# Widening the vector block behind x from 66 to 80 columns, so that what follows it in SBUF starts at a multiple of 64 bytes

## The chip, the cores and the metric

The kernel runs on one core of one Trainium2 chip. Its time is the device time of one execution in microseconds; the time before is the median of three executions. A profiled execution on the same core gives the trace that all readings come from. The core's engines are TensorE (PE, with its weight loads listed apart as PEld), VectorE (DVE), ScalarE (ACT), GpSimd (POOL) and SyncE (SP, which issues nearly all DMAs).

## The reference, cut to what matters

One decoder layer on x of 512 tokens by 1024 channels, all in float32: a half-step SwiGLU feed-forward block, a mixer that runs a gated linear recurrence and a stick-breaking attention side by side, and a second feed-forward block.

```
x = x + 0.5 * swiglu(rms_norm(x, ffn1_norm), w_gate, w_up, w_down)      # 1024 -> 2816 -> 1024
h = rms_norm(x, mix_norm);  proj = h @ w_in                              # 1024 -> 2560
y_rnn = rg_lru(...);        y_att = stick_breaking(q, k, v)              # 8 heads of 64
x = x + concat(norm(y_rnn), norm(y_att)) @ w_out                         # 1024 -> 1024
x = x + 0.5 * swiglu(rms_norm(x, ffn2_norm), w_gate, w_up, w_down)
```

## The kernel before

x is kept transposed: eight tiles `x0` to `x7` of 128 channels by 512 tokens. All small vectors (norm gains, convolution weights, biases) stand as columns in one block `vec`, which shares the first tile with x's first block: `x0` is 512 + `NVEC` float32 columns wide (lines 121 to 123) and comes with one DMA (line 547).

Products of float32 accuracy are made from parts. A matrix W is split on the chip into a high part, rounded to the float32r type by ACT, and a low part, the rest, by DVE (`weights` and `parts`, lines 126 to 136). An activation is split in the same way (`Normed.add` for x's parts `xh` and `xl`, `split` for the hidden layer's `hh` and `hl`). One product is then three matmuls into the same accumulator (`mm3`, lines 142 to 145):

```
nc.tensor.matmul(out_, wh, ah, start=start, stop=False)
nc.tensor.matmul(out_, wh, al, start=False, stop=False)
return nc.tensor.matmul(out_, wl, ah, start=False, stop=stop)
```

Each matmul loads a stationary operand of 128 columns (PEld) and streams a moving operand of 512, 384, 256 or 128 columns past it (PE).

The stages in order of time:

- `first_products` (lines 532 to 587): gate and up products of the first three column blocks of the first feed-forward block. Its weights have buffers of their own (`first_r`, `first_h`, `first_l`), all from a pool that opens behind x's parts. For each k, six matmuls follow each other with the same moving part of x and six weights into six accumulators: 3 x 8 x 6 = 144 matmuls at line 580.
- `ffn` (lines 221 to 522), called for "a" and "b". Column blocks 0 to 5 are plain (`products`, through `mm3`; "a" makes only three there). The other 16 blocks are made in pairs by `fast`: a Strassen-like scheme of seven half products (`matrix`, `product`, line 397), whose moving operand is 256 columns wide, or 512 for some of the matmuls where the pair is "wide" (`WIDE`, line 38). A narrow matrix has 7 x 12 matmuls of 256 columns, a wide one 7 x 4 of 512 and 7 x 4 of 256. Each of the two blocks has ten wide and six narrow matrices. `down` multiplies by the third weight matrix in chunks of 6, 6, 6 and 4 blocks; eight down blocks of 18 matmuls stand between the half products of the next pairs (`BETWEEN`, line 34) for the second and third chunk, the others stand by themselves. The last down block of "b" is cut into 384 and 128 columns.
- The mixer: `project` (moving operand is x's parts, stationary the weights), `project_qkv` (the other way round: x's parts are stationary, the weights move), `gate`, `turn`, the attention (`weigh`, `turn_weights`, `attend`) and the output projection (`weigh_out`, moving operands `yrh`, `yrl`, `yah`, `yal`, which use the buffers of x's parts).

PE's order is written out in the program, and the trace has PE in that order throughout. DVE and ACT prepare parts ahead, with four buffers for each of the weights' parts.

Tiles are placed in SBUF one behind the other, pool by pool, and each starts at a multiple of 32 bytes. The kernel's own allocation, in bytes of each partition:

| what | starts at | modulo 64 | modulo 128 |
|---|---|---|---|
| weights' high parts `h_` (wpool, four buffers) | 31424, 35520, 39616, 43712 | 0 | 64 |
| weights' low parts `l_` (wpool, four buffers) | 47808, 51904, 56000, 60096 | 0 | 64 |
| `x0`, 578 columns, 2312 bytes | 64192 | 0 | 64 |
| `x1` to `x7`, every 2048 | from 66528 | 32 | 96 |
| x's parts `xh`, `xl`, every 2048 | from 80864 | 32 | 96 |
| weights of `first_products`, every 4096 | from 122080 | 32 | 96 |
| `hh`, `hl` of the feed-forward blocks, every 4096 | from 142560 | 32 | 96 |
| last byte in use | 228576 | | |

The pools behind `x0` (x's parts, the statistics, `first`, the feed-forward pools, the mixer's q and k parts, the attention's tiles) all have such starts. An exception is the recurrence's pool, where a tile of 2060 bytes (`xr`) turns what lies behind it (`xch`, `xcl`, `nat`, `gel` and others) back to 0 modulo 64.

Of the kernel before, what the change touches and what calls it, by code (L numbers as in the profile page):

```python
# [15 lines left out]
P = 128  # L16
# [30 lines left out]
C_G1, C_GM, C_G2 = 0, 8, 16  # L47
C_CW, C_CB, C_BA, C_BX, C_LAM = 24, 40, 44, 48, 52
C_RN, C_AN, C_QN, C_KN = 56, 60, 64, 65
NVEC = 66  # L50


@with_exitstack
def hybrid_layer_kernel(
# [65 lines left out]

    x0 = xpool.tile([P, T + NVEC], F32, tag="x0", name="x0")
    vec = x0[:, T:]
# [409 lines left out]
    def first_products():  # L532

        with tc.tile_pool(name="first", bufs=1, reuse_waits="tile") as fi:
# [8 lines left out]
            for kk in range(KD // 2):  # L543
                s = slice(2 * kk * P, (2 * kk + 2) * P)
                c = 2 * kk * T + NVEC
                if kk == 0:
                    nc.sync.dma_start(x0, xT[:, : T + NVEC])
                else:
# [562 lines left out]
def _layout(x, ffn1_norm, ffn1_w_gate, ffn1_w_up, ffn1_w_down, mix_norm, w_in,  # L1111
            conv_w, conv_b, rg_w_a, rg_b_a, rg_w_x, rg_b_x, rg_lambda,
            q_norm, k_norm, rnn_out_norm, attn_out_norm, w_out,
            ffn2_norm, ffn2_w_gate, ffn2_w_up, ffn2_w_down):
    import numpy as np

    def cols(v):
        return np.asarray(v).reshape(-1, P).T

    def by_block(w):  # L1120

        k, n = w.shape
        return w.reshape(k // P, P, n // P, P).transpose(2, 1, 0, 3).reshape(n // P, P, k)

    def by_pairs(w):


        o = by_block(w).reshape(NF, P, KD, P)
        o = np.concatenate([o[:, :, 0::2], o[:, :, 1::2]], axis=2).reshape(NF, P, KD * P)
        o = np.concatenate([o[1::2], o[0::2]], axis=2)  # L1130
        b = by_block(w)
        o[: PLAIN // 2] = np.concatenate([b[0:PLAIN:2], b[1:PLAIN:2]], axis=2)
        return o

    w = np.asarray(w_in)[0]
    qkv = w[:, 2 * DR :].reshape(KD // 2, 2, P, 3, DR).transpose(3, 0, 2, 1, 4)
    def gates(a, x):

        a, x = np.asarray(a)[0], np.asarray(x)[0]
        o = np.empty((P, NJ, P), a.dtype)  # L1140
        for n in range(2 * NJ):
            r = (n % 2) * HD
            o[r : r + HD, n // 2, r : r + HD] = a[n]
            o[r : r + HD, n // 2, HD - r : 2 * HD - r] = x[n]
        return o.reshape(P, NJ * P)

    def swapped(v):

        return np.asarray(v).reshape(-1, 2, HD)[:, ::-1].reshape(-1)

    vecs = np.concatenate(
        [
            cols(ffn1_norm[0]), cols(mix_norm[0]), cols(ffn2_norm[0]), cols(conv_w[0]),
            cols(conv_b[0]), cols(rg_b_a[0]), cols(swapped(rg_b_x[0])), cols(rg_lambda[0]),
            cols(rnn_out_norm[0]), cols(attn_out_norm[0]),
            cols(np.tile(np.asarray(q_norm[0]), 2)), cols(np.tile(np.asarray(k_norm[0]), 2)),
        ],
        axis=1,
    )

    xt = np.asarray(x)[0].T.reshape(KD, P, T).transpose(1, 0, 2).reshape(P, KD * T)
    a = {
        "xT": np.concatenate([xt[:, :T], vecs, xt[:, T:]], axis=1),
        "w_rg": by_block(w[:, : 2 * DR]),
        "w_qkv": qkv.reshape(3, KD // 2, P, 2 * DR),
        "w_gate": gates(rg_w_a, rg_w_x),
        "w_out": by_block(np.asarray(w_out)[0]),
        "wg1": by_pairs(np.asarray(ffn1_w_gate)[0]),
        "wu1": by_pairs(np.asarray(ffn1_w_up)[0]),
        "wd1": by_block(np.asarray(ffn1_w_down)[0]),  # L1170
        "wg2": by_pairs(np.asarray(ffn2_w_gate)[0]),
        "wu2": by_pairs(np.asarray(ffn2_w_up)[0]),
        "wd2": by_block(np.asarray(ffn2_w_down)[0]),
    }
    return {n: np.ascontiguousarray(a[n]) for n in _INS}
# [21 lines left out]
```

## Time and profile before

| | us |
|---|---|
| median of three executions | 909.22 (908.8 to 909.35) |
| the profiled execution | 908.92 |
| its span, first to last instruction | 907.1 |
| PE busy | 901.0 (99%) |
| PE loading weights | 758.1 (84%) |
| DVE busy | 712.9 (79%) |
| ACT busy | 466.9 (51%) |
| POOL busy | 72.9 (8%) |
| mean granted TensorE clock | 1.000 |

The 1.8 us between the profiled execution and its span lie around the program's instructions. Matmuls are pipelined: the duration of one (0.39 us at 512 columns) is longer than the distance from its start to the next start. The time that a matmul really takes from the kernel is that distance, called spacing below, and it is read from start times.

### The profile page before, as it was taken

What the parts mean: (1) busy time and instruction counts of PE and PEld (TensorE: products, weight loads), DVE (VectorE), ACT (ScalarE), POOL (GpSimd) and SP (SyncE); (2) the same over time, 40 slices, a digit from 0 to 9 for tenths busy, and PEclk for the clock granted to TensorE, in tenths of its full rate; (3) what the DMA queues carried; (4) which work ended last, traced back from release to release, by engine and by line L of the source; (5) the groups of instructions that cost most, each with busy time, mean ns of one, the idle gap of its engine ahead of it and who ended that gap; (6) DMA issues with size and microseconds to landing.
All of it is one profiled execution on the core that took longest, in us unless ns stands there. A gap on an engine that the chain in (4) does not pass through costs nothing.

```text
span 907.1 us, 12596 instructions
## 1 busy us (share of the span) xinstructions
PE 901.0 (99%) x4880; PEld 758.1 (84%) x4880; DVE 712.9 (79%) x1032; ACT 466.9 (51%) x771; POOL 72.9 (8%) x60
## 2 busy tenths in 40 slices
PE   9999999999999999999999999999999999999998
PEld 7888899888988888877887678888899888998887
DVE  8598789887887669758689959697689967896763
ACT  7254365544653446365768844445256534563450
POOL 0000000000000005544140001400000000000000
PEclk9999999999999999999999999999999999999999
DMA  8323322331232222322132002324322332233202
GB/s 284 106 62 138 115 93 93 133 141 53 94 128 93 76 93 83 115 72 103 58 116 71 25 24 94 117 66 149 117 93 93 120 129 78 93 112 99 88 24 92
DMA packets 27452, 89.18 MB, mean 98 GB/s; under 512 B 2817, under 2 KB 6145, under 8 KB 23297
## 3 DMA queue, kind: packets, MB, share of 16 engines
q1 hardware_dynamic: 27248, 88.26, 29.0%
q8 instruction: 38, 0.62, 0.3%
q14 instruction: 22, 0.17, 0.1%
q10 hardware_dynamic: 144, 0.13, 0.0%
HBM read 86.28 MB, written 2.10 MB: 97 GB/s over the span
## 4 chain that ended last, share of the span: by engine, by line
PE 98%; DVE 1%; DMA 0%; issue 0%; ACT 0%; DVEq 0%
PE pxua L397 5%; PE pxub L397 5%; PE pxgb L397 5%; PE pxga L397 5%; PE pdb L144 5%; PE pdb L145 5%; PE pdb L143 5%; PE pda L144 5%; PE pda L145 5%; PE pda L143 5%; PE pyua L397 4%; PE pyga L397 4%; PE pygb L397 4%; PE pyub L397 4%; PE first_p L580 4%; PE po L143 2%
## 5 line engine op out<-in xcount | busy, mean ns | idle before, releaser
L144 PE MATMUL pdb<-hlb,h_db 128*128 128x512 f32 (+2 forms) x180 | 70.1, 391 | 0.0
L145 PE MATMUL pdb<-hhb,l_db 128*128 128x512 f32 (+2 forms) x180 | 69.7, 391 | 0.0
L143 PE MATMUL pdb<-hhb,h_db 128*128 128x512 f32 (+2 forms) x180 | 69.3, 391 | 0.0
L144 PE MATMUL pda<-hla,h_da 128*128 128x512 f32 x176 | 69.2, 395 | 0.0
L145 PE MATMUL pda<-hha,l_da 128*128 128x512 f32 x176 | 68.9, 395 | 0.0
L143 PE MATMUL pda<-hha,h_da 128*128 128x512 f32 x176 | 68.0, 395 | 0.0
L482 DVE SCALAR_TENSOR_TENSOR x<-pdb,x 128x512 f32<-128x512 f32 (+2 forms) x33 | 21.9, 673 | 35.8 <-PE pdb L145 35.8
L133 ACT CAST h_da<-r_da 128x768 fp32r<-128x768 f32 (+1 forms) x28 | 24.2, 867 | 43.5 <-PE pda L144 21.4
L133 ACT CAST h_db<-r_db 128x768 fp32r<-128x768 f32 (+1 forms) x28 | 24.2, 868 | 41.3 <-PE pdb L144 21.8
L482 DVE SCALAR_TENSOR_TENSOR x<-pda,x 128x512 f32<-128x512 f32 x32 | 21.6, 687 | 27.2 <-PE pda L145 27.2
L145 PEld LDWEIGHTS pdb<-hhb,l_db 128*128 128x128 f32 x180 | 33.8, 188 | 7.7
L144 PEld LDWEIGHTS pdb<-hlb,h_db 128*128 128x128 f32 x180 | 33.8, 188 | 7.2
L143 PEld LDWEIGHTS pdb<-hhb,h_db 128*128 128x128 f32 x180 | 33.8, 188 | 6.9
L145 PEld LDWEIGHTS pda<-hha,l_da 128*128 128x128 f32 x176 | 33.0, 187 | 7.9
L144 PEld LDWEIGHTS pda<-hla,h_da 128*128 128x128 f32 x176 | 33.0, 187 | 7.3
L143 PEld LDWEIGHTS pda<-hha,h_da 128*128 128x128 f32 x176 | 33.0, 188 | 7.1
L173 POOL TENSOR_TENSOR sqa_m<-sqa_m,sq_m 128x512 f32<-128x512 f32 x7 | 11.8, 1681 | 312.4 <-ACT sq_m L172 312.2
L377 ACT CAST h_gb<-rgb 128x512 fp32r<-128x512 f32 (+1 forms) x24 | 18.4, 765 | 24.2 <-PE pdb L144 12.8
L135 DVE TENSOR_TENSOR l_da<-r_da,h_da 128x768 fp32r<-128x768 f32 (+1 forms) x28 | 27.7, 989 | 2.9 <-ACT h_da L133 2.9
L135 DVE TENSOR_TENSOR l_db<-r_db,h_db 128x768 fp32r<-128x768 f32 (+1 forms) x28 | 27.7, 992 | 2.9 <-ACT h_db L133 2.9
L377 ACT CAST h_ua<-rua 128x512 fp32r<-128x512 f32 (+1 forms) x24 | 18.3, 764 | 22.5 <-PE pyga L397 8.8
L377 ACT CAST h_ub<-rub 128x512 fp32r<-128x512 f32 (+1 forms) x24 | 18.4, 765 | 22.1 <-PE pygb L397 8.8
(459 smaller groups left out, 2821.3 us busy)
## 6 DMA issues: line engine op xcount, KB each, us to landing
r_da<-in_wd SPq DMA_DIRECT2D x24, 384.0 KB, 3.1
r_db<-in_wd SPq DMA_DIRECT2D x24, 384.0 KB, 3.1
rga<-in_wg SPq DMA_DIRECT2D x8, 1024.0 KB, 5.7
rua<-in_wu SPq DMA_DIRECT2D x8, 1024.0 KB, 4.7
rgb<-in_wg SPq DMA_DIRECT2D x8, 1024.0 KB, 5.0
rub<-in_wu SPq DMA_DIRECT2D x8, 1024.0 KB, 4.8
r_o<-in_w_out SPq DMA_DIRECT2D x8, 512.0 KB, 3.5
r_gb<-in_wg SPq DMA_DIRECT2D x6, 512.0 KB, 3.8
```

Of the source, the lines that this page charges most:

```text
L133: nc.scalar.copy(hi, raw)
L135: nc.vector.tensor_sub(lo, raw, f32(hi))
L143: nc.tensor.matmul(out_, wh, ah, start=start, stop=False)
L144: nc.tensor.matmul(out_, wh, al, start=False, stop=False)
L145: return nc.tensor.matmul(out_, wl, ah, start=False, stop=stop)
L173: (engine or nc.gpsimd).tensor_add(self.acc, self.acc, sq)
L377: nc.scalar.copy(hi[:, to], a)
L397: nc.tensor.matmul(pt[:, : r.shape[1]], l[:, s], r, start=start and (k, i) == order[0], stop=(k, i) == order[-1], skip_group_check=True,)
L482: nc.vector.scalar_tensor_tensor(x[k][:, t], pt[:, t], 0.5, x[k][:, t], op0=ALU.mult, op1=ALU.add)
L580: nc.tensor.matmul(pts[i], wp[i][:, s], xp[k], start=k == 0 and wp is hi and xp is n1.h, stop=k == KD - 1 and wp is lo,)
```

## The change

`NVEC` becomes 80, and 14 columns of zeros are added to the array of vectors. `x0` is then 592 columns, 2368 bytes, 37 x 64, and `x1` starts at 64192 + 2368 = 66560 bytes, 0 modulo 64. Everything placed behind it moves on by 32 bytes. The DMA of `x0` carries 128 x 2368 bytes in place of 128 x 2312, and the later columns of x are found 14 columns further on (line 545). No instruction is added or taken out, and nobody reads the zeros.

```diff
 C_RN, C_AN, C_QN, C_KN = 56, 60, 64, 65
-NVEC = 66
+NVEC = 80
...
             cols(conv_b[0]), cols(rg_b_a[0]), cols(swapped(rg_b_x[0])), cols(rg_lambda[0]),
             cols(rnn_out_norm[0]), cols(attn_out_norm[0]),
             cols(np.tile(np.asarray(q_norm[0]), 2)), cols(np.tile(np.asarray(k_norm[0]), 2)),
+            np.zeros((P, NVEC - C_KN - 1), np.float32),
         ],
         axis=1,
     )
```

## The prediction

> **What bounds the kernel.** I read the page's parts 1 and 4 first, then PE's timeline stage by stage. Busy time, and after it the shares of the chain that ended last:
>
> ```profile
> PE 901.0 (99%) x4880; PEld 758.1 (84%) x4880; DVE 712.9 (79%) x1032; ACT 466.9 (51%) x771; POOL 72.9 (8%) x60
> PE 98%; DVE 1%; DMA 0%; issue 0%; ACT 0%; DVEq 0%
> ```
>
> PE is never without work and the chain is PE itself. A faster feed buys nothing; only the spacing of matmuls does, so spacing is what I read next. PE's timeline in the first stage (start, duration of the merged row, matmuls in it):
>
> ```profile
> 18.09 1.52 PE L580 MATMUL first_p<-xh_a,first_h 128*128 128x512 f32 x6
> 33.05 1.52 PE L580 MATMUL first_p<-xh_a,first_l 128*128 128x512 f32 x6
> 34.41 0.95 PE L180 MATMUL pst_a<-ones,sqa_a 128*128 128x1 f32 x8
> 35.22 1.65 PE L580 MATMUL first_p<-xh_a,first_h 128*128 128x512 f32 x6
> 36.70 1.54 PE L580 MATMUL first_p<-xl_a,first_h 128*128 128x512 f32 x6
> 38.08 1.52 PE L580 MATMUL first_p<-xh_a,first_l 128*128 128x512 f32 x6
> 39.44 0.60 PE L200 MATMUL psr_a<-ident,r_a 128*128 128x128 f32 x4
> ```
>
> From 18.09 to 33.05 lie 66 matmuls: 0.2267 us each. Now the same shape after that stage: plain products up to the first down block, and the q projection, where the operands have changed places:
>
> ```profile
> 40.57 0.40 PE L143 MATMUL pga<-xh_a,h_ga 128*128 128x512 f32 x1
> 73.47 0.39 PE L143 MATMUL pda<-hha,h_da 128*128 128x512 f32 x1
> ...
> 377.45 0.40 PE L144 MATMUL pq<-l_q,xh_m 128*128 128x512 f32 x1
> 386.08 0.40 PE L145 MATMUL pq<-h_q,xl_m 128*128 128x512 f32 x1
> ```
>
> 40.57 to 73.47 are 141 matmuls (144 of three plain blocks, less the three before 40.57): 0.2333 us each. 377.45 to 386.08 are 37: 0.2332. The half products, from the chain in order of time:
>
> ```profile
> 115.66 1.40 PE pxua L397 x12
> 117.06 1.40 PE pyua L397 x12
> ...
> 132.45 1.40 PE pxga L397 x8
> 133.85 1.17 PE pyga L397 x6
> ```
>
> Twelve of 256 columns take 1.40 us, 0.1167 each; a wide row of four at 512 and four at 256 also takes 1.40, that is 0.2333 and 0.1167. So there are two speeds for one shape: 6.67 ns (2.9%) less in the first stage than in all others, at the same granted clock:
>
> ```profile
> core 0: 907.1 us, clock 1.000
> ```
>
> **What goes with the faster speed.** By the allocation, stationary and moving operand start alike modulo 64 only in the first stage (32 and 32). The plain products have 0 and 32, the q projection 32 and 0, the half products and down blocks 0 and 32. Three other things are special there: six matmuls in a row share a moving tile, accumulators rotate, and weights lie in other buffers. The restart at 35.22 speaks against the first two: there the moving tile repeats and accumulators rotate from the first matmul on, yet six take 36.70 - 35.22 = 1.48 us, the next six 1.38, and only then 39.44 - 38.08 = 1.36. After a break the stage runs about ten matmuls at the slow spacing, losing 0.14 us against 1.36 + 1.36, some 0.09 of it in the one longer first step, and then snaps to the fast one. The start of the kernel does the same with two moving tiles in turn:
>
> ```profile
> 7.88 0.39 PE L580 MATMUL first_p<-xh_a,first_l 128*128 128x512 f32 x1
> 8.57 0.39 PE L580 MATMUL first_p<-xh_a,first_h 128*128 128x512 f32 x1
> 8.80 0.39 PE L580 MATMUL first_p<-xl_a,first_h 128*128 128x512 f32 x1
> 9.02 1.07 PE L580 MATMUL first_p<-xh_a,first_l 128*128 128x512 f32 x4
> 9.93 1.52 PE L580 MATMUL first_p<-xh_a,first_h 128*128 128x512 f32 x6
> ```
>
> Three at 0.230 (7.88 to 8.57), then 0.23, 0.22 and four at 0.2275, although xh and xl alternate at 8.57, 8.80 and 9.02. I read it as two streams that settle into step when they start alike modulo 64, and that lose one 64-byte step (16 float32 columns; 6.67 ns is 2.9% of 233 ns, 16 of 544 columns) per matmul when they are 32 apart. That is an inference: the trace has no float32r matmul of 512 columns with both operands at 0.
>
> **The change, part by part.**
>
> *Matmuls of 512 columns.* The change makes 0/32 and 32/0 into 0/0. From the loops: plain products 144 + 288, down blocks 1056 less 12 that are cut, `project` 192, output projection 192, half products 560, `project_qkv` 288: 2708 matmuls. At 6.67 ns each, 18.1 us. All lie on the path, since PE is the path. The ends are nothing and, if the new pair is out of step by a further step, 18.1 us more; I take the gain, as the first stage is the nearest row.
>
> *Matmuls of 256 columns.* 20 wide matrices give 28 and 12 narrow ones 84: 1568. No row shows them in step. The slow spacings stand 2 to 1 like the columns, so I take half of 6.67, 3.33 ns, 5.2 us. The ends are 0 (the weight load may set the pace: 84% of the span has one running) and the full step, 10.5 us.
>
> *Restarts.* Each break in the stream costs some ten matmuls of settling: 0.14 - 0.09 = 0.05 us. A restart is seen as a first matmul of 0.48 us:
>
> ```profile
> 39.80 0.48 PE L143 MATMUL pga<-xh_a,h_ga 128*128 128x512 f32 x1
> 365.50 0.48 PE L143 MATMUL pxr<-xh_m,h_xr 128*128 128x512 f32 x1
> 584.41 0.48 PE L143 MATMUL pub<-xh_b,h_ub 128*128 128x512 f32 x1
> ```
>
> Between the first and the last of these I count 33 in PE's start times, nearly all in the mixer: 1.6 us of the gain is lost. No product at 512 columns restarts between 40 and 365.
>
> *Who must keep up.* The stream would run 2.9% faster, so parts must be ready and accumulators free 2.9% earlier. Busy time by stretch (length, then PE, PEld, DVE, ACT, POOL, clock, DMA share, GB/s):
>
> ```profile
> 35.00:107.00 72.00, 72.00 (x314) 58.02 (x314) 60.58 (x105) 29.25 (x51) 1.02 (x1) 1.00 0.30 99
> 107.00:187.00 80.00, 80.00 (x528) 72.75 (x528) 68.75 (x100) 47.95 (x80) 0.00 (x0) 1.00 0.27 95
> 340.00:355.00 15.00, 15.00 (x66) 12.06 (x65) 13.91 (x16) 10.00 (x15) 8.22 (x5) 1.00 0.18 54
> 475.00:545.00 70.00, 68.26 (x469) 51.42 (x468) 55.18 (x53) 48.78 (x108) 1.01 (x1) 1.00 0.12 44
> ```
>
> DVE has 68.75 us of work where PE would need 77.7, and 13.91 where it would need 14.6. The cover holds, thinnest in the last down blocks before the mixer, where DVE also writes x's parts. I allow 0.7 us of new waits. If DVE's cover were gone, the most would be the gain of the stretches where it is over 85% busy (the second and third row): 95 us x 2.9% = 2.7 us. SP issues no more DMAs than before; transfers take a third of the DMA engines' time or less in these stretches. In the attention (475 to 545) DVE and ACT set much of the pace, and I count no gain beyond its output products.
>
> *First transfer.* x's first part waits for `x0`:
>
> ```profile
> x<-in_xT SPq DMA_DIRECT2D x7, 256.0 KB, 4.0
> x<-in_xT SPq DMA_DIRECT2D x1, 289.0 KB, 3.7
> 4.45 0.72 ACT L157 ACTIVATE xh_a<-x 128x512 fp32r<-128x512 f32 x1 [1.78 <-DMA x<-in_xT]
> ```
>
> It grows by 7 KB, 2.4% of 3.7 us: at most 0.09 us later. The smaller ones take longer, so size hardly decides and it may cost nothing. I take 0.05.
>
> *ACT and DVE on moved tiles.* Making x's parts from `x0` (at 0) and from `x1` (at 32) costs the same:
>
> ```profile
> 5.35 0.75 DVE L159 SCALAR_TENSOR_TENSOR xl_a<-x,xh_a 128x512 fp32r<-128x512 f32 x1
> 8.34 0.75 DVE L159 SCALAR_TENSOR_TENSOR xl_a<-x,x,xh_a 128x512 fp32r<-128x512 f32 x1 [0.17 <-ACT xh_a L157]
> ```
>
> 0.75 us both times, so moving the tiles costs these engines nothing. The recurrence's tiles go the other way, from 0 to 32, while `gate_h` goes from 32 to 0: its 24 matmuls stay 32 apart. The first stage goes from 32/32 to 0/0; if that were not the same, its 144 matmuls cost 1.0 us.
>
> Sum: -18.1 - 5.2 + 1.6 + 0.7 + 0.05 = -21.0, from 908.9 for the profiled execution, which stands 0.3 us under the median: **888 us**, 2.3% faster.
>
> By the Trainium skill, "TensorE: Matmul & The Clock Gate", section "Wait — 56ns, not 53.3ns?", bf16 matmuls of 512 columns follow each other at 215.7 ns. No stage here reaches it; if 0/0 did, 2708 x 17.6 ns would be an estimated 48 us.
>
> **The rivals.**
>
> *Nothing changes.* The speed may come from where the first stage's weights lie: its buffers are far from the four that all other weights use, at 31424 to 64192, and every slow stage has one operand in those. The change doesn't touch that. For it: no row separates place from residue. Against it: each slow stage pairs those buffers with other tiles, and the slow spacing is the same to 0.1 ns whichever operand is the weights. Time 909. The same page, section "Step-by-step: what each phase is for", says that loading the next weights takes nothing from the running matmul's reads, through a port of their own; by that rule start addresses would not matter, and this rival is its outcome. The trace disagrees at least on there being one speed.
>
> *Only long, uniform streams settle.* Settling took some ten matmuls, and half products change accumulator, tiles and often width every 8 to 12. Then L397 stays as it is, and with it the 2 x 2 x 144 down matmuls between: 2708 - 560 - 576 = 1572 at 6.67 ns, 10.5 less 1.6 us: 900. Against it: the steps at 9.02 and 9.93 change tiles without losing it.
>
> *Slower.* The true period may be 128 bytes. The weights' buffers are at 64 modulo 128 and x's parts would be at 0, opposite; in the first stage both are at 96. The place is every product stage, and the price is one more step: spacing 0.240 and 0.120, 2708 x 6.67 + 1568 x 3.33 ns = 23 us, 932. It decides from a spacing above 0.2333. Against it: 64 bytes is just the step lost per matmul, so slipping should reach it.
>
> **How the numbers follow.** In step everywhere 0.50; only long streams 0.16; nothing 0.26; slower 0.08. A measurement of this kernel can tell about 0.2%, 1.8 us, from no change. Faster 0.66, same 0.26, slower 0.08. The likeliest case alone reaches from 883 (256 columns gain the full step) to 896 (they gain nothing and DVE's cover fails). The range takes in the rivals up to no change, 883 to 911, leaving out the slower case and some of the tails.
>
> **What would show it.** Right: plain products, down blocks and the q projection at 0.227 like the first stage, PE's busy time near 880 and its share still 99%, half products of twelve at about 1.36. Wrong: 1.40 for six of 512 columns outside the first stage (no change), 1.44 (slower), the gain in plain stages alone (long streams), or new idle time of PE on `l_` or `h_` parts (the cover).

## The result and the profile after

The changed kernel takes 898.46 us (median of four, 898.36 to 898.6) beside 909.04 for the kernel before (four, 908.8 to 909.35): ratio 0.9884, 95% interval 0.9869 to 0.99. It is faster by 10.6 us, half of the 21 forecast. The profiled span went from 907.1 to 896.7 us, 10.4 less, at a granted clock of 1.000.

Of the page's parts 1 and 4 of the kernel after, the busy time of each engine and the shares of the chain that ended last:

```profile
PE 891.0 (99%) x4880; PEld 757.9 (85%) x4880; DVE 712.4 (79%) x1032; ACT 466.2 (52%) x771; POOL 72.9 (8%) x60
PE 98%; DVE 1%; DMA 0%; issue 0%; ACT 0%; DVEq 0%
```

PE lost 10.0 us of busy time and is still the whole chain; the other engines work as long as before. So the gain is in the spacing of matmuls, and only there. PE's timeline after, with start, duration and count of matmuls: two rows of the first stage, then the plain products and the q projection:

```profile
21.98 1.52 PE L580 MATMUL first_p<-xh_a,first_h 128*128 128x512 f32 x6
32.86 1.52 PE L580 MATMUL first_p<-xh_a,first_l 128*128 128x512 f32 x6
...
40.40 0.39 PE L143 MATMUL pga<-xh_a,h_ga 128*128 128x512 f32 x1
73.59 0.39 PE L144 MATMUL pda<-hla,h_da 128*128 128x512 f32 x1
...
373.15 0.39 PE L143 MATMUL pq<-h_q,xh_m 128*128 128x512 f32 x1
381.55 0.39 PE L143 MATMUL pq<-h_q,xh_m 128*128 128x512 f32 x1
```

The first stage has 48 matmuls between its two rows, 10.88 us, 0.2267 each as before. The plain products have 145 in 33.19 us: 0.2289, where the forecast said 0.2267 and the kernel before had 0.2333. The q projection has 36 in 8.40 us: 0.2333, no gain at all. A third value, 0.2289, exists that the trace before did not show. One by one, in the same timeline:

```profile
76.11 0.39 PE L143 MATMUL pda<-hha,h_da 128*128 128x512 f32 x1
76.34 0.39 PE L144 MATMUL pda<-hla,h_da 128*128 128x512 f32 x1
76.56 0.39 PE L145 MATMUL pda<-hha,l_da 128*128 128x512 f32 x1
76.79 0.39 PE L143 MATMUL pda<-hha,h_da 128*128 128x512 f32 x1
```

Three steps take 0.68 us. Three of the fast kind take 0.680 and three of the slow kind 0.700; averaged over the stream the three are 0.687, which is a loss of 6.67 ns in three matmuls where the kernel before lost three times that.

The half products in the chain in order of time (start, length, count of matmuls):

```profile
108.55 1.41 PE pxua L397 x12
109.96 1.41 PE pyua L397 x12
111.38 1.38 PE pxga L397 x8
...
128.09 1.36 PE pxua L397 x12
129.45 1.36 PE pyua L397 x12
```

Wide rows gained a little, 1.40 to 1.38. Rows of twelve at 256 columns come in two kinds: 1.36, which is just the half step that was forecast (12 x 3.33 ns = 0.04 us less than 1.40), and 1.41, slightly slower than before. Of the 70 that stand by themselves in the chain, 22 take 1.36 and 48 take 1.41; before, all 70 took 1.40 to 1.42. The wide rows have the same two kinds, but there each kind suits one shape: of the 104 that stand by themselves, with four matmuls of each shape, 46 have their 256s at 113.3 ns in the mean and their 512s at 231.9, the other 58 have 117.7 and 228.5. So the two gains of the forecast never come together in a wide row, and both kinds come to about 1.38 us.

Summed over start times, stage by stage: the 2708 matmuls of 512 columns outside the first stage went from 635.09 to 625.79 us, 9.30 less; the 1568 of 256 columns from 183.10 to 182.12, 0.97 less. Together 10.27 of the 10.4 us of the span.

### The profile page after: what moved, and what is told of

Read it like the earlier page. It is cut to its first block, busy times and chain, and to the rows that moved or that the text cites. A ratio compares the mean times of both kernels' runs of the same rounds, so it can differ in the third digit from the quotient of the medians.

```text
span 896.7 us, 12596 instructions
## 1 busy us (share of the span) xinstructions
PE 891.0 (99%) x4880; PEld 757.9 (85%) x4880; DVE 712.4 (79%) x1032; ACT 466.2 (52%) x771; POOL 72.9 (8%) x60
## 4 chain that ended last, share of the span: by engine, by line
PE 98%; DVE 1%; DMA 0%; issue 0%; ACT 0%; DVEq 0%
PE pxub L397 5%; PE pxua L397 5%; PE pxga L397 5%; PE pxgb L397 5%; PE pdb L145 5%; PE pdb L143 5%; PE pdb L144 5%; PE pda L145 5%; PE pda L143 5%; PE pda L144 4%; PE pyub L397 4%; PE pyua L397 4%; PE pygb L397 4%; PE pyga L397 4%; PE first_p L580 4%; PE po L143 2%
```

## The experiments

The first reading after the result: what counts is the distance from the stationary tile's start to the moving tile's, modulo 256 bytes, not whether both have the same residue modulo 64. By the allocation, modulo 256, the weights are at 192 in both kernels. x's parts were at 224 before, distance +32, and are at 0 after, distance +64; in the q, k and v projections, where the operands have changed places, it is -32 and -64; in the first stage it is 0 in both kernels. The rivals: the residue of one operand alone, and the place of the first stage's buffers. All edits are against the kernel before, and where `NVEC` grows, zeros fill the array of vectors as in the change.

**Distance 0.** `w128` puts x's parts at 192 as well.

```diff
-NVEC = 66
+NVEC = 128
```

> The vector block is 128 columns wide, so x's parts start exactly a multiple of 256 bytes from the weights' parts (0 modulo 256, as in the first stage), in place of 64 bytes past such a multiple as after the change. Distance theory (the spacing depends on the distance from stationary to moving operand modulo 256, and 0 is the pair in step): products of 512 columns and the q, k, v projections at 0.227 us outside the first stage, 256 columns at 0.113 to 0.117, 884 to 890 us. Period of 64 bytes (alike modulo 64 is all that counts, and what is missing is lost elsewhere): as after the change, 898.5 us. Place theory (only the first stage's buffers are fast): 898.5 us, since no buffer changes its neighbourhood.

Measured: 900.74 us beside 908.87, ratio 0.9912 (0.9895 to 0.9928). Its timeline, plain products and q projection:

```profile
40.70 0.39 PE L143 MATMUL pga<-xh_a,h_ga 128*128 128x512 f32 x1
73.58 0.39 PE L144 MATMUL pda<-hla,h_da 128*128 128x512 f32 x1
...
374.98 0.39 PE L143 MATMUL pq<-h_q,xh_m 128*128 128x512 f32 x1
383.14 0.39 PE L143 MATMUL pq<-h_q,xh_m 128*128 128x512 f32 x1
```

145 matmuls in 32.88 us and 36 in 8.16: 0.2268 and 0.2267. The weights lie where they lay, so the first stage's speed is not a matter of its buffers' place, and the q projection gains like the others once its distance is 0. This much went as the theory of distance said. The time did not, since the 256-column matmuls of the half products became slower than before, which no theory had expected. Its chain in order of time:

```profile
108.26 1.43 PE pxua L397 x12
109.69 1.44 PE pyua L397 x12
```

All 1568 of 256 columns now take 186.92 us, against 183.10 before and 182.12 after. Matmuls of 256 columns do better at another distance than those of 512.

**Distances 128 and -64.** `w96` and `w112`:

```diff
-NVEC = 66
+NVEC = 96     # w96: distance 128
+NVEC = 112    # w112: distance -64
```

> The vector block is 96 columns wide: x's parts start 128 bytes past a multiple of 256 from the weights' parts, 0 modulo 128. Period of 128 bytes: as good as a distance of 0, 884 to 890 us, q, k, v projections at 0.227 too. Distance modulo 256: a third value that no run has shown yet, between 888 and 909 us, the same for the projections of q, k and v as for the others, since 128 and -128 are the same. Period of 64 bytes: 898.5 us.

> The vector block is 112 columns wide: x's parts start 192 bytes past a multiple of 256 from the weights' parts, that is -64 where the change has +64. Distance modulo 256: the two kinds of product change places: the products with x's or the hidden layer's parts as moving operand return to 0.2333 us, the q, k, v projections go to 0.229; 907 to 909 us. Period of 128 bytes: 64 and -64 are the same, 898.5 us. Period of 64 bytes: 898.5 us.

Measured: w96 910.15 us, ratio 1.0014 (1.0004 to 1.0023); w112 904.05, ratio 0.9947 (0.9932 to 0.9962). The timeline of w96, then that of w112 in the same plain products:

```profile
40.55 0.39 PE L143 MATMUL pga<-xh_a,h_ga 128*128 128x512 f32 x1
73.55 0.41 PE L144 MATMUL pda<-hla,h_da 128*128 128x512 f32 x1
```

```profile
41.99 0.40 PE L143 MATMUL pga<-xh_a,h_ga 128*128 128x512 f32 x1
69.06 0.40 PE L145 MATMUL pga<-xh_a,l_ga 128*128 128x512 f32 x1
```

142 in 33.00 us, 0.2324, and 116 in 27.07, 0.2334. Distances 0, 64, 128 and -64 are all alike modulo 64 and give four spacings, so the period is over 64 bytes; 0 differs from 128, so it is not 128 either. A period of 256 fits all runs: the starts in the first stage before and in w128 differ by 256 and by 0 modulo 512, and both have 0.2267. w96 came out 1 us above the 909 that the forecasts allowed, with the 256-column matmuls slower again (185.77 us). w112 lies 3 us under its 907 to 909: it is faster than before, with no gain in its plain products, by the half products above all; its chain in order of time:

```profile
111.44 1.36 PE pxua L397 x12
112.80 1.36 PE pyua L397 x12
```

Of the 70 rows of twelve here, 66 take 1.36 or 1.37: the 256-column matmuls sum to 178.78 us, the best of all distances.

**x's parts at 0 modulo 64, distance kept.** `pad32` moves the weights by 32 bytes too, through a tile ahead of them, with `NVEC` at 66.

```diff
-    warm = const.tile([P, 8], F32, tag="warm", name="warm")
+    warm = const.tile([P, 16], F32, tag="warm", name="warm")[:, :8]
```

> The vector block has its 66 columns as before, and 32 bytes are left free ahead of all weights' buffers: x's parts and the hidden layer's lie at 0 modulo 64, the weights' parts at 32 modulo 64, with the distances between them as before the change. If only the distance counts: 909 us, 0.2333 us everywhere but in the first stage, where both operands are now at 0 and 0.2267 us stays. If the start of the moving operand at 0 modulo 64 counts by itself: 898.5 us or less.

Measured: 908.78 us, ratio 0.9998 (0.9989 to 1.0008). The plain products in its timeline:

```profile
40.83 0.40 PE L143 MATMUL pga<-xh_a,h_ga 128*128 128x512 f32 x1
67.89 0.40 PE L145 MATMUL pga<-xh_a,l_ga 128*128 128x512 f32 x1
```

116 in 27.06 us: 0.2333. x's parts lie at 0 modulo 64 as the change has them, and nothing is gained. So it is the distance that counts, and not the residue of the moving operand alone.

The mean spacings by distance, from start times (ns; steps over 270 ns, which are breaks in the stream, are left out):

| distance, bytes | kernel | plain 512 | q, k, v 512 (sign turned) | 256 | median, us |
|---|---|---|---|---|---|
| +32 | before | 233.3 | 233.3 | 116.8 | 908.9 |
| +64 | after | 229.0 | 233.3 | 116.1 | 898.46 |
| 128 | w96 | 232.6 | 232.6 | 118.5 | 910.15 |
| -64 | w112 | 233.3 | 230.5 | 114.0 | 904.05 |
| 0 | w128 | 226.9 | 227.2 | 119.2 | 900.74 |

The second sign agrees in part: q, k, v at +64 in w112 reach 230.5 in the mean (its q projection alone stays at 233.0), and at -64 in the kernel after 233.3.

**Each shape at its own distance.** `half64` takes 0 for all plain streams and -64 for the half products, by moving their weights 64 bytes into wider buffers. One tile of the statistics shares another's buffer to make room.

```diff
+NVEC = 128
+WB = KD * P + 64
+SHIFT = 16
-                    hi = wpool.tile([P, width], F32R, tag="wh", name=f"h_{n}{group}", bufs=4)
+                    hi = wpool.tile([P, WB], F32R, tag="wh", name=f"h_{n}{group}", bufs=4)[:, SHIFT : SHIFT + width]
...   # lo and the buffers in parts() likewise
-            rb = stat.tile([P, T], F32, tag="rb", name=f"rb_{n}", bufs=1)
+            rb = stat.tile([P, T], F32, tag="sq", name=f"rb_{n}")
```

> The vector block is 128 columns wide, which gives the plain products, down blocks and projections a distance of 0 from stationary to moving operand; the half products' weights alone start 64 bytes (16 columns) further on in their buffers, which gives them a distance of -64. The weights' buffers are 256 bytes longer each, and the normalisation's spread factors share two buffers with the squares so that all fits. Distance theory, each shape with an optimum of its own: matmuls of 256 columns go from 0.1192 us at distance 0 to 0.1140, those of 512 columns in half products from 0.231 to 0.232, all else stays as at distance 0: 900.7 - 1568 x 5.2 ns + 560 x 1.4 ns = 893.4 us, faster than the change. If the 256-column spacing in the run with 112 columns came from something else than the weights' distance (the whole pool had moved there): 900.7 us.

Measured: 894.5 us beside 908.83, ratio 0.9847 (0.9832 to 0.9861). Timeline and chain of it, in this order (L146 is mm3's first matmul here, L400 the half product):

```profile
40.67 0.39 PE L146 MATMUL pga<-xh_a,h_ga 128*128 128x512 f32 x1
73.55 0.39 PE L147 MATMUL pda<-hla,h_da 128*128 128x512 f32 x1
```

```profile
108.24 1.36 PE pxua L400 x12
109.60 1.36 PE pyua L400 x12
```

145 in 32.88 us, 0.2268, beside twelves of 1.36: both shapes are near their best in one kernel. Not all of it: 17 of its 70 rows of twelve still take 1.41 or 1.42. Eight of the ten that come right behind a down block are among them, and the same eight take 1.36 or 1.37 in w112, whose down blocks have the distance of its half products. The 256-column matmuls sum to 179.82 us, the half products of 512 columns stay slow (232.9 ns). This is the fastest kernel of all, 4 us below the change.

**Half products at -32 and -96.** `half32` and `half96` are half64 with `SHIFT = 8` and `SHIFT = 24`.

> As the one before with the half products' weights 32 bytes (8 columns) further on: distance -32, not tried yet at 256 columns. Distance theory in steps of 16 cycles: anything from 0.1133 us (no step lost) to 0.1200 (one in each), 892 to 902 us. If all distances that are 32 off a multiple of 64 act alike: 0.1167 as before the change, with 512 columns at 0.2333, 898 us.

> As the one before with the half products' weights 96 bytes (24 columns) further on: distance -96, not tried yet. Distance theory: anything from 0.1133 to 0.1200 us for 256 columns, 892 to 902 us. If all distances that are 32 off a multiple of 64 act alike: 0.1167, 898 us, like the run with 32 bytes.

Measured: 901.49 us (ratio 0.9919, 0.9899 to 0.9939) and 900.36 (0.9907, 0.9887 to 0.9927), each from two runs (902.57 and 900.41; 900.41 and 900.32). The 256-column spacing is 118.5 and 118.3 ns, where +32 had 116.8 in the kernel before: distances that are 32 off a multiple of 64 are not alike, and of the seven distances run -64 alone brings most rows of 256 columns to 1.36. The plain matmuls beside them are at 0 here and were at +32 before, so the neighbours differ too.

**Half products of 512 columns at 0.** In half64 these are the one shape left at a bad distance. `wide0` gives the high parts of wide matrices, which alone have such matmuls, the distance 0 again; `half64b` is half64 beside it.

```diff
+                    HS = 0 if wide else SHIFT
-                    hi = wpool.tile(...)[:, SHIFT : SHIFT + width]
+                    hi = wpool.tile(...)[:, HS : HS + width]
```

> As the run with the half products' weights 64 bytes further on, but the high parts of wide matrices, whose matmuls have 512 columns, stay at distance 0; their low parts (256 columns) and all narrow matrices keep -64. If each matmul follows its own shape and distance: the 560 matmuls of 512 columns go from 0.2329 back to 0.2310 us, 1 us less, 893.4. If what counts is the load beside it (the second of two neighbours decides) or if changing distances cost steps, as with the low parts moved alone: no gain, 894.5 us or some tenths more.

> The run with the half products' weights 64 bytes further on once more, beside the one before on the same chip: 894.5 us by every theory.

Measured: wide0 897.92 us (0.9886, 0.9868 to 0.9903), half64b 894.37 (0.984, 0.9824 to 0.9856). Wide0's chain in order of time:

```profile
108.20 1.41 PE pxua L401 x12
109.61 1.42 PE pyua L401 x12
```

The 512s gained 1.3 us (130.41 to 129.12), and the 256s lost 4.9 (179.82 to 184.68): 66 of the 70 rows of twelve take 1.41 or 1.42, though the narrow matrices' weights are where half64 has them. So what comes before a matmul counts as well as its own distance, as behind the down blocks of half64.

**What meets what.** While a matmul streams, the next weights load. Is the disturbance between the moving tile and its own weights, or the next ones'? `lows32` puts a gap of 32 bytes between the high and the low weights, so that x's parts are at 0 to the high and -32 to the low ones.

```diff
+NVEC = 120
...   # spaced = [] ahead of it
+        if not spaced:      # once, between the first high and the first low buffer
+            spaced.append(wpool.tile([P, 8], F32, tag="wgap", name="wgap", bufs=1))
...   # and filled with zeros
```

> The low parts of all weights but the first stage's lie 32 bytes further on than the high parts; x's and the hidden layer's parts are at distance 0 from the high parts and -32 from the low ones (the vector block is 120 columns wide for that). In each product of three matmuls the third has the low part as stationary operand. If the running matmul meets the load of the next weights: the step is lost in the second matmul, which runs while the low part is loaded, so the spacing after line 144 is near 0.2333 us and those after lines 143 and 145 near 0.2267. If it meets its own stationary operand: the spacing after line 145 is the long one. Either way a third of 1860 matmuls loses 6.67 ns, about 4 us over the run with 128 columns, and the half products shift by something unknown: 900 to 907 us. If only x's parts and the high parts matter: 0.2267 in all three.

Measured: 910.44 us, ratio 1.0023 (1.0014 to 1.0033), outside what either theory gave for the time. The timeline, where L148, L149 and L150 are mm3's three matmuls:

```profile
76.19 0.40 PE L148 MATMUL pda<-hha,h_da 128*128 128x512 f32 x1
76.42 0.40 PE L149 MATMUL pda<-hla,h_da 128*128 128x512 f32 x1
76.66 0.39 PE L150 MATMUL pda<-hha,l_da 128*128 128x512 f32 x1
76.89 0.40 PE L148 MATMUL pda<-hha,h_da 128*128 128x512 f32 x1
```

The long step, 0.24, follows L149: its own weights are high, at distance 0, and the low ones load beside it. Over all these products the steps after the three lines are 232.4, 237.6 and 229.1 ns in the mean. The place of the long step speaks for the next weights' load. But the three together come to 233.0 a matmul, 233.3 in the plain products, so two good distances in three saved next to nothing.

`load64` makes that load shorter: the kernel before, with only the first 64 of 128 stationary columns in the down blocks. It leaves out half of each down product, and only half of x's rows are updated.

```diff
-                            mm3(pt[:, t], wh[:, s], wl[:, s], hs[i][0][:, t], ...)
+                            mm3(pt[: P // 2, t], wh[:, s][:, : P // 2], wl[:, s][:, : P // 2], hs[i][0][:, t], ...)
```

> The kernel before, with only the first 64 of the 128 stationary columns in all down blocks, so that half of each down product is left out and the loads of weights there are half as long; distance 32 as before. If the steps are lost where the running matmul reads beside the load of the next weights: the spacing of down matmuls of 512 columns falls below 0.2333 us, to 0.2267 or less, about 7 us or more over 1044 matmuls, while plain products stay at 0.2333. If the moving operand alone loses them, by its own place: 0.2333 in the down blocks too, 909 us.

Measured: 906.86 us in one run, span 905.1. The group of weight loads in the kernel before, by line and form (busy time, mean ns of one, idle time before), the same in load64, and two rows of load64's timeline:

```profile
L143 PEld LDWEIGHTS pda<-hha,h_da 128*128 128x128 f32 x176 | 33.0, 188 | 7.1
```

```profile
L143 PEld LDWEIGHTS pda<-hha,h_da 128*64 128x64 f32 x176 | 23.7, 135 | 14.7
```

```profile
342.82 0.40 PE L144 MATMUL pda<-hla,h_da 128*64 128x512 f32 x1
346.97 0.39 PE L144 MATMUL pda<-hla,h_da 128*64 128x512 f32 x1
```

The load takes 135 ns in place of 188. The 18 matmuls between the two rows take 4.15 us, 0.2306 each; over all down blocks the mean is 231.0 against 233.3 before, and the plain products of the same run, with full loads, stay at 233.3. That fits a part of the load in the lost time, but 28% less load gave back only 2.3 of 6.67 ns, where the theory that it is the whole cause had expected 0.2267 or less. The edit also halves the columns that the matmul itself uses, and no run parts the two. How moving operand and load meet is not settled.

## Why the prediction was right in direction and half in size

- *What bounds the kernel*: right. PE's share stayed 99%, and 10.27 of 10.4 us are spacing.
- *What goes with the faster speed*: this step failed. "Alike modulo 64" fits the trace of before, where only the distances +32, -32 and 0 occur, but it is not the rule: the spacing goes by the distance modulo 256 bytes (w128, w96, w112, pad32). The change made +64 and -64, not 0. The forecast read "0 and 0 modulo 64" off the allocation, although the same table gave the weights 64 modulo 128 and x's parts 96, which the change makes 0: the "slower" rival held that fact, with the wrong price. That this change gained is in part luck: w96 and w112 put the same tiles at 0 modulo 64 too, so by the forecast's rule they would also have come to 888 us, and they took 910.15 and 904.05.
- *512 columns, -18.1 us*: measured -9.30. Plain products, down blocks, `project` and the output projection gained 3.6 to 4.3 ns each in steady spacing, in place of 6.67, half products of 512 columns 3.3 (130.60 to 128.77 us for 560), q, k and v nothing.
- *256 columns, -5.2 us*: measured -0.97. The half step was the right size for rows that reach it (1.36), but only 22 of 70 did at this distance; in w112, at -64, 66 do.
- *Restarts, +1.6 us*: the count stayed: 31 of the 2708 steps are longer than 0.27 us before, and 31 after. Settling looks as forecast. After the break in the first stage, in the timeline after:

```profile
35.03 1.65 PE L580 MATMUL first_p<-xh_a,first_h 128*128 128x512 f32 x6
36.52 1.54 PE L580 MATMUL first_p<-xl_a,first_h 128*128 128x512 f32 x6
37.90 1.52 PE L580 MATMUL first_p<-xh_a,first_l 128*128 128x512 f32 x6
```

  1.49 us for the first six and 1.38 for the next, as 1.48 and 1.38 before. What restarts cost of the measured gain lies inside the two sums above and was not measured apart.
- *Who must keep up, +0.7 us*: nothing. DVE's cover held, and all of PE's waits of 0.3 us or more, in the view of waits, are at the start and in the attention. The waits, and then the stretch of half products by windows (columns as in the prediction):

```profile
PE warm L529 <- DVE ones L101: 1.1, 1, 1.1
PE py L1012 <- DVE yal L1027: 0.8, 1, 0.8
...
PE py L1012 <- ACT wt L1004: 0.3, 1, 0.3
```

```profile
105.60:183.00 77.40, 77.40 (x518) 70.96 (x517) 66.67 (x98) 46.20 (x78) 0.00 (x0) 1.00 0.29 98
```

  DVE has 66.67 us of work in 77.40, 86%: enough room for another 2% of spacing, as half64 then showed.
- *First transfer, +0.05 us*: no loss. The first part of x is made earlier than before, at 4.13 against 4.45, in the timeline after:

```profile
4.13 0.72 ACT L157 ACTIVATE xh_a<-x 128x512 fp32r<-128x512 f32 x1 [1.46 <-DMA x<-in_xT]
```

- *ACT and DVE on moved tiles*: DVE's 712.9 became 712.4, ACT's 466.9 became 466.2. No cost.
- *The rivals*: "nothing" fell with w128, which reaches 0.2268 with the weights in their old buffers. By the Trainium skill, "TensorE: Matmul & The Clock Gate", section "Step-by-step: what each phase is for", the load of the next weights takes no SBUF read bandwidth from the running matmul. That leaves the spacing's dependence on the starts unexplained, and two runs speak against a load that costs nothing: lows32 changed nothing in the products but starts and made the step beside the low weights' load the longest (237.6 ns), and load64 shortened the load and with it the spacing (233.3 to 231.0), though not the load alone. "Only long streams" came out near the measured time, 900, for a wrong reason: the long uniform q projection gained nothing, while half products of 512 columns did. "Slower" is false at 128 as well: w96 has 0.2324, not 0.240.
- *The range*: by its own terms the likeliest case ends at 895 (908.9 - 18.1 + 1.6 + 2.7 + 0.05), not 896; nothing hangs on it.

## What to carry to other kernels

Where TensorE is the path and matmuls follow each other without idle time, compare the spacing of one shape over all stages before anything else: two values at one clock can be a gain that costs no work, and here they came from the start addresses of moving and stationary tiles. Two speeds in one trace fit many rules; list the exact starts modulo several powers of two, and let one kernel move both operands (pad32) and one reproduce the good pair fully (w128) before trusting the simplest one. Choose the distance for each shape and keep it the same through long stretches: 0 for the plain matmuls and -64 bytes for the half products gave 894.4 us here, and mixing distances within one product lost 3.5 us of that gain (wide0) or, by another mix, all of it (lows32).

## What the runs showed that was not expected

- The spacing of 512-column float32r matmuls has at least four values, 226.7 to 233.3 ns, by the distance modulo 256 bytes; moving both operands by 32 bytes had no effect (pad32).
- Matmuls of 256 columns prefer another distance: 114.0 ns at -64 and 119.2 at 0, the best distance for 512. Why is open.
- At one distance there can be two lasting spacings: twelves of 1.36 and of 1.41 us in the kernel after. Row by row, the order of the two kinds is the same in both feed-forward blocks, so it follows from the program and not from chance; what in it chooses was not tried.
- The long step falls where the low weights load and not where they are used (lows32), and down matmuls on half the columns, with a load that is 28% shorter, took back a third of the lost time (load64). Why the period is 256 bytes stays open.
